# Hybrid attention/mLSTM block on one core: PSUM banks dealt out anew, weight tiles loaded two units ahead, gate products in four groups, small loads in another order

## The chip, the cores and the metric

The kernel runs on one core of one Trainium2 chip. The metric is the device time of one execution in microseconds (us). Of the kernel before there are three runs, with a median of 1435.84 us (1435.15 to 1436.73). One further execution was profiled. In this text PE is the matrix engine, DVE the vector engine, ACT the scalar engine, POOL the general-purpose engine and SP the engine that issues most DMAs.

## What is computed

One layer of a block with sequence length S = 1024 and width D = 1024, in float32. `x` is normalised (RMSNorm) and multiplied by one wide input matrix, whose columns feed two branches. Eight heads of differential attention: two softmaxes per head, with a bias that depends on the distance of the positions and a mask by chunks of 64, of which the second times lambda is taken from the first before the product with v. And eight heads of an mLSTM (a matrix memory with gates). Both are gated, projected, merged by per-channel gates, projected once more, added to `x` and normalised again. The attention, cut to what matters here:

```python
logits = jnp.einsum("pbhqd,pbhkd->pbhqk", qb, k).astype(jnp.float32) + bias
probs = jax.nn.softmax(jnp.where(mask, logits, NEG_INF), axis=-1)
attn = probs[0] - lam * probs[1]
return jnp.einsum("bhqk,bhkv->bhqv", attn, v)
```

## The kernel before

**Split numbers.** TensorE works on fp16 pairs. Each float32 operand is split into a high and a low half, and each product is three matmuls: L329 to L331 with 512 columns, where the weights stand still (q, k and others), and L358 to L360 with 256 columns, where `x` stands still.

**Units.** The input projection is cut into units of up to 256 weight columns. A unit's weights come from HBM in two halves of four k-chunks, `wt`, from a pool of WT = 3 tiles (L44, L223). `prep` (L234) sums their squares on ACT (L245), `fnorm_finish` (L155) turns the sum into a scale by way of a tiny matmul (L165) and a row of one-column DVE operations (L135 to L139), and the scaled halves are written as `wp` by ACT (L257) and DVE (L259). `start_load` asks for a unit's first half and `finish_load` for the second.

**The order.** Python generators write instructions down in an interleaved order, and a scheduler with the tile pools decides what finally stands in each engine's queue. The main loop (L1067 to L1116) goes through the units, and between a unit's matmuls it takes steps of a side job by a table of slots: PLAN_A for attention heads 0 to 6, PLAN_C for head 7, PLAN_M, PLAN_N and PLAN_Z for the mLSTM heads.

**An attention head** (L797). It has eight blocks of 128 queries. For block i and each of two halves, PE writes logits to `psb` (L812, one tile of two PSUM banks), DVE adds the bias BB and takes the extreme (L822), and ACT takes exp (L826). `combine` subtracts the two (L837 on DVE), and `turn` splits the result (L844 on ACT, L845 on DVE) and has a DMA on SP's queue transpose it (L847). `pv` (table names v0 to v7, L855 to L857) multiplies the transposed tile with v into `pvp`: blocks 0 to 3 fill one PSUM bank, and 4 to 7 the next one. ACT sums the squares of the result (L858), POOL makes a factor (L862 to L864, `fac`), and DVE reads the bank out, scaled by it (`on`, L870). `pvp` has one bank, so that v4 starts when L870 has read blocks 0 to 3. Q and K of the next head come from its own unit by way of `hl` (L599, L600) and four small DMAs each (L608, L610).

**Before the first head.** `x` arrives in eight tiles. ACT and DVE sum their squares (L383, L381), DVE scales them (L387), PE transposes them (L396, into `pmi`, two banks), and ACT and DVE write the pair X (L398, L399). The bias table `tb` is written to DRAM with one copy for each of 128 rows (`tb_d`, L432, 1.57 MB out of 8 partitions). A head's `strip` is read back from it (L584) and scaled by POOL (L585, L588), and DVE copies it into BB (L800). The input and forget gates of the mLSTM need 32 matmuls with a stationary operand of 32 columns (L468).

## Time and profile before

| what | value |
|---|---|
| three runs | 1435.84 us median (1435.15 to 1436.73) |
| the profiled execution | 1435.78 us, of which the span is 1433.9 us |
| PE busy | 1380.6 us (96% of the span) |
| DVE, ACT, POOL busy | 848.0, 735.0, 157.5 us |
| granted TensorE clock, mean | 0.995 |

The span runs from the first to the last instruction that the profile shows; 1.9 us of the execution lie outside it. In a list of instructions a row has its start, its duration, the engine and line, what is written and read, and in brackets the idle time of its engine just before it with what ended that. In the list of waits a row has the engine, the tile and line that waited, what it waited for, and then the total in us, the number of times and the longest.

### The profile page before, as it was taken

What the parts mean: (1) busy time and instruction counts of PE and PEld (TensorE: products, weight loads), DVE (VectorE), ACT (ScalarE), POOL (GpSimd) and SP (SyncE); (2) the same over time, 40 slices, a digit from 0 to 9 for tenths busy, and PEclk for the clock granted to TensorE, in tenths of its full rate; (3) what the DMA queues carried; (4) which work ended last, traced back from release to release, by engine and by line L of the source; (5) the groups of instructions that cost most, each with busy time, mean ns of one, the idle gap of its engine ahead of it and who ended that gap; (6) DMA issues with size and microseconds to landing.
All of it is one profiled execution on the core that took longest, in us unless ns stands there. A gap on an engine that the chain in (4) does not pass through costs nothing.

```text
span 1433.9 us, 25050 instructions
## 1 busy us (share of the span) xinstructions
PE 1380.6 (96%) x9650; PEld 913.3 (64%) x9650; DVE 848.0 (59%) x2310; ACT 735.0 (51%) x1533; POOL 157.5 (11%) x215
## 2 busy tenths in 40 slices
PE   6989999999999999999999999999999999999997
PEld 3656575665756655444486787778769675444786
DVE  6276868677686756533445674775866564233633
ACT  7276556565566667832353444443435344644542
POOL 2001010010100100100102020220211200122004
PEclk9999999999999999999999999999999999999999
DMA  6456355463554645543321313231232135534303
GB/s 200 68 142 140 83 107 124 104 141 82 114 121 91 136 95 130 163 149 125 96 74 60 104 31 101 47 87 47 66 97 75 60 86 158 168 103 162 118 16 118
DMA packets 232585, 150.14 MB, mean 105 GB/s; under 512 B 117297, under 2 KB 209730, under 8 KB 232466
## 3 DMA queue, kind: packets, MB, share of 16 engines
q1 hardware_dynamic: 218450, 123.28, 35.0%
q10 hardware_dynamic: 14016, 25.27, 5.3%
q8 instruction: 75, 1.23, 0.3%
q14 instruction: 44, 0.36, 0.1%
HBM read 90.12 MB, written 18.55 MB: 76 GB/s over the span
## 4 chain that ended last, share of the span: by engine, by line
PE 77%; DVE 9%; ACT 4%; DMA 4%; POOL 3%; issue 3%; SPq 0%; POOLq 0%; DVEq 0%; ACTq 0%
PE pp L329 14%; PE pp L331 14%; PE pp L330 14%; PE pp L360 8%; PE pp L358 8%; PE pp L359 8%; PE psb L812 3%; DVE z L822 3%; DMA z<-z 2%; ACT z L826 1%; DMA qw<-rows_d 1%; DVE wp L259 1%; PE psb L908 1%; PE pvp L855 1%; DVE hl L600 1%
## 5 line engine op out<-in xcount | busy, mean ns | idle before, releaser
L358 PE MATMUL pp<-wp,X 128*128 128x256 f16 x1280 | 349.7, 273 | 0.0
L359 PE MATMUL pp<-wp,X 128*128 128x256 f16 x1280 | 349.7, 273 | 0.0
L360 PE MATMUL pp<-wp,X 128*128 128x256 f16 x1280 | 349.7, 273 | 0.0
L329 PE MATMUL pp<-X,wp 128*128 128x512 f16 x768 | 291.7, 380 | 0.3 <-ACT wp L257 0.3
L331 PE MATMUL pp<-X,wp 128*128 128x512 f16 x768 | 291.3, 379 | 0.6 <-DVE wp L259 0.6
L330 PE MATMUL pp<-X,wp 128*128 128x512 f16 x768 | 291.8, 380 | 0.0
L257 ACT ACTIVATE wp<-wt,sb 128x512 f16<-128x512 f32 x208 | 136.9, 711 | 105.4 <-DVE sb L138 70.6
L331 PEld LDWEIGHTS <-wp 128*128 128x128 f16 x1024 | 100.0, 98 | 119.7 <-DVE wp L259 1.2
L245 ACT ACTIVATE junk<-wt 128x1024 bf16<-128x1024 f32 x112 | 118.1, 1055 | 100.0 <-DMA wt<-in_w_in_dram 89.7
L329 PEld LDWEIGHTS <-wp 128*128 128x128 f16 x1024 | 100.2, 98 | 103.0 <-issue 1.7
L330 PEld LDWEIGHTS <-wp 128*128 128x128 f16 x1024 | 100.1, 98 | 97.1
L259 DVE SCALAR_TENSOR_TENSOR wp<-wt,sb,wp 128x512 f16<-128x512 f32 x208 | 150.5, 760 | 14.4 <-ACT wp L257 12.8
L359 PEld LDWEIGHTS <-X 128*128 128x128 f16 x1280 | 125.3, 98 | 18.4 <-issue 2.4
L358 PEld LDWEIGHTS <-X 128*128 128x128 f16 x1280 | 125.4, 98 | 16.8 <-issue 0.8
L360 PEld LDWEIGHTS <-X 128*128 128x128 f16 x1280 | 125.3, 98 | 14.6
L826 ACT ACTIVATE z<-z,mx 128x256 f32<-128x256 f32 (+7 forms) x128 | 99.0, 773 | 61.7 <-DVE mx L825 46.1
L822 DVE CUSTOM_DVE_ANT_0 z<-psb,BB,negc 128x256 f32<-128x256 f32 (+7 forms) x128 | 104.1, 813 | 19.7 <-PE psb L812 19.4
L331 PE MATMUL pp<-Y,wp 128*128 128x512 f16 x256 | 97.1, 379 | 0.0
L330 PE MATMUL pp<-Y,wp 128*128 128x512 f16 x256 | 97.1, 379 | 0.0
L329 PE MATMUL pp<-Y,wp 128*128 128x512 f16 x256 | 97.1, 379 | 0.0
L649 DVE SCALAR_TENSOR_TENSOR acc<-up,wcol,acc 128x512 f32<-128x512 f32 x96 | 78.0, 827 | 27.4 <-POOL acc L650 24.5
L812 PE MATMUL psb<-K,Q 128*128 128x512 f16 (+3 forms) x384 | 83.5, 326 | 7.8 <-DMA K<-hl 4.6
(245 smaller groups left out, 2012.1 us busy)
## 6 DMA issues: line engine op xcount, KB each, us to landing
wt<-in_w_in_dram SPq DMA_DIRECT2D x128, 256.0 KB, 3.4
wt<-in_w_in_dram SPq DMA_DIRECT2D x24, 512.0 KB, 3.9
K<-hl SPq DMA_DIRECT2D x32, 256.0 KB, 3.7
gate_d<-tg ACTq DMA_DIRECT2D x32, 256.0 KB, 2.2
xt<-in_x_dram SPq DMA_DIRECT2D x8, 512.0 KB, 5.2
Q<-hl SPq DMA_DIRECT2D x32, 128.0 KB, 2.4
wt<-in_w_pa_dram SPq DMA_DIRECT2D x8, 512.0 KB, 5.4
ft<-gate_d ACTq DMA_DIRECT2D x16, 256.0 KB, 2.8
```

What stands on the lines that cost most here:

```text
L245: s.activation(j, w.wt[k], AF.Square, accum_out=ss[:, k:k + 1])
L257: s.activation(dst[0], src, AF.Copy, scale=w.sb)
L259: v.scalar_tensor_tensor(dst[1], src, w.sb, dst[0], op0=ALU.mult, op1=ALU.subtract)
L329: te.matmul(ps, wh, xh, start=(start and i == 0), stop=False, **kw)
L330: te.matmul(ps, wh, xl, start=False, stop=False, **kw)
L331: te.matmul(ps, wl, xh, start=False, stop=(stop and i == n - 1), **kw)
L358: te.matmul(ps[:, o], xh[:, t], wh, start=i == 0, stop=False)
L359: te.matmul(ps[:, o], xh[:, t], wl, start=False, stop=False)
L360: te.matmul(ps[:, o], xl[:, t], wh, start=False, stop=i == KC - 1)
L812: te.matmul(sp[:, c:e], Q[:, p, i * P:(i + 1) * P], K[p][:, j, c:e], start=(j == 0), stop=(j == 1))
L822: v.tensor_tensor_reduce(z[:, :n], sp[:, :n], bb[:, S - n:], negc, BIG, op0=ALU.add, op1=ALU.min, accum_out=mx)
L826: s.activation(z[:, :n], z[:, :n], AF.Exp, bias=mx, scale=-1.0, accum_out=rr[:, 2 * i + p:2 * i + p + 1])
```

## The change

- PSUM: `pmi` goes from two banks to one and `pvp` from one to two. The transposes of `x`, and in the mLSTM the small transposes and state products, take `pvp` instead of `pmi`.
- PLAN_A has v6 two slots and v7 four slots later in the table.
- Weights: WT goes from 3 to 6. The main loop finishes the load of the next unit and starts that of the one after it; unit 2 is loaded ahead of the main loop.
- `prep` waits five steps instead of two between the sums of squares and their use. For the first unit DVE takes one of the two sums, and of the first four tiles of `x` it takes tile 3 instead of tile 1.
- The strip is asked for and scaled after the four transfers of K. Its masked corner is written as 0 times strip plus a constant, without the tile `maskv`.
- The gate products go to four groups of 32 partitions of one PSUM bank, by half of the sequence and by high or low part of X. One ACT copy takes them out, the result goes to DRAM by ACT's queue, and `if_gates` loads six pieces instead of four and adds the two more on DVE.

Names in the diff: `te`, `s`, `v`, `g` are PE, ACT, DVE, POOL; `m_ps`, `v_ps`, `s_ps` take a tile of `pmi`, `pvp`, `psb`.

```diff
 RING = 15
-PLAN_A = [(0, 'q0'), (0, 'r0'), (0, 'q1'), (3, 'r1'), (4, 'q2'), (5, 'r2'), (9, 'q3'), (9, 'r3'), (9, 'q4'), (10, 'v0'), (14, 'v1'), (16, 'r4'), (17, 'q5'), (18, 'v2'), (19, 'r5'), (21, 'q6'), (24, 'r6'), (25, 'q7'), (27, 'r7'), (28, 'v3'), (29, 'v4'), (29, 'v5'), (30, 'f0'), (30, 'o0'), (31, 'v6'), (31, 'v7'), (42, 't0'), (55, 'f1'), (55, 'o1'), (55, 't1')]
+PLAN_A = [(0, 'q0'), (0, 'r0'), (0, 'q1'), (3, 'r1'), (4, 'q2'), (5, 'r2'), (9, 'q3'), (9, 'r3'), (9, 'q4'), (10, 'v0'), (14, 'v1'), (16, 'r4'), (17, 'q5'), (18, 'v2'), (19, 'r5'), (21, 'q6'), (24, 'r6'), (25, 'q7'), (27, 'r7'), (28, 'v3'), (29, 'v4'), (29, 'v5'), (30, 'f0'), (30, 'o0'), (33, 'v6'), (35, 'v7'), (42, 't0'), (55, 'f1'), (55, 'o1'), (55, 't1')]
...
 T2 = 5
-WT = 3
+WT = 6
 AHEAD = 2
...
     psb = ctx.enter_context(tc.tile_pool(name="psb", bufs=1, space=PSUM))
-    pmi = ctx.enter_context(tc.tile_pool(name="pmi", bufs=2, space=PSUM))
-    pvp = ctx.enter_context(tc.tile_pool(name="pvp", bufs=1, space=PSUM))
+    pmi = ctx.enter_context(tc.tile_pool(name="pmi", bufs=1, space=PSUM))
+    pvp = ctx.enter_context(tc.tile_pool(name="pvp", bufs=2, space=PSUM))
...
     g.memset(BB, 0.0)
-    maskv = ctile([64, 64], p="maskv")
-    g.memset(maskv, -(2.0 ** 100))
...
-    def prep(w, rowscale=None, keep=False):
+    def prep(w, rowscale=None, keep=False, alone=False):
         wd = w.width
...
         for k in range(2):
-            j = junk(4 * wd).rearrange("p (a b) -> p a b", a=4)
-            s.activation(j, w.wt[k], AF.Square, accum_out=ss[:, k:k + 1])
-            yield
-        yield
-        yield
+            if alone and k:
+                flat = w.wt[k].rearrange("p a b -> p (a b)")
+                v.tensor_tensor_reduce(main_tile("junk").bitcast(BF), flat, flat, 1.0, 0.0, op0=ALU.mult, op1=ALU.add,
+                                       accum_out=ss[:, k:k + 1])
+            else:
+                j = junk(4 * wd).rearrange("p (a b) -> p a b", a=4)
+                s.activation(j, w.wt[k], AF.Square, accum_out=ss[:, k:k + 1])
+            yield
+        for _ in range(5):
+            yield
         w.sb = sm(p="sb")
...
                 self.finish_load()
-                self.prepping = prep(self.w, self.rowscale and self.rowscale(), self.keep)
-                self.left = 16
+                self.prepping = prep(self.w, self.rowscale and self.rowscale(), self.keep, self is first)
...
             ss = sm(p="xss")
-            if tt in (1,):
+            if tt == (1 if th else 3):
                 v.tensor_tensor_reduce(main_tile("junk").bitcast(BF), xt, xt, 1.0, 0.0, op0=ALU.mult, op1=ALU.add, accum_out=ss)
...
                 X[th, kc // 2] = xtile("X")
-            tp = m_ps()
+            tp = v_ps()
             for tt in range(4):
-                te.transpose(tp[:, tt * P:(tt + 1) * P], xts[th * 4 + tt][:, kc * P:(kc + 1) * P], ident)
+                xb = xts[th * 4 + tt][:, kc * P:(kc + 1) * P]
+                te.transpose(tp[:, tt * P:(tt + 1) * P], xb, ident)
             hi, lo = x_src(kc, th)
...
     wsc = ctile([P, NT, H], p="wsc")
-    gif_d = dram.tile([32, S], F32, tag="gifd", name="gif_d")
+    gif_d = dram.tile([P, 512], F32, tag="gifd", name="gif_d")
...
             yield
-        t = R(shape=[32, S], p="gif")
-        for th in range(2):
-            gps = m_ps()
-            for i in range(KC):
+        t = R(shape=[P, 512], p="gif")
+        gps = s_ps()[:, :512]
+        for i in range(KC):
+            for th in range(2):
                 for k in range(2):
-                    te.matmul(gps[:32, :], parts[:, i, :], x_src(i, th)[k], start=(i + k == 0),
-                              stop=(i + k == KC))
-                yield
-            s.activation(t[:, HS[th]], gps[:32, :], AF.Copy, scale=sig[:32, :])
-        nc.sync.dma_start(gif_d, t)
+                    o = (th * 2 + k) * 32
+                    te.matmul(gps[o:o + 32, :], parts[:, i, :], x_src(i, th)[k], start=(i == 0), stop=(i == KC - 1))
+            yield
+        s.activation(t, gps, AF.Copy, scale=sig)
+        s.dma_start(gif_d, t)
         yield
...
         ff = R(shape=[H, NT, P], p="ff")
-        gl = [R(shape=[H, NT, P], p="gl") for _ in range(2)]
-        for k, dst in ((0, gi), (1, ff), (2, gl[0]), (3, gl[1])):
-            nc.sync.dma_start(dst.rearrange("h a b -> h (a b)"), gif_d[k * H:k * H + H, :])
+        gl = [R(shape=[H, NT, P], p="gl") for _ in range(4)]
+        for k, dst in ((0, gi), (1, ff), (2, gl[0]), (3, gl[1]), (4, gl[2]), (5, gl[3])):
+            r = k * H if k < 4 else 32 + (k - 4) * H
+            nc.sync.dma_start(dst.rearrange("h (t a) b -> h t (a b)", t=2),
+                              gif_d.rearrange("(t r) c -> r t c", t=2)[r:r + H])
         for _ in range(4):
...
             v.scalar_tensor_tensor(dst, dst, bif[:, k:k + 1], gl[k], op0=ALU.add, op1=ALU.add)
+            v.tensor_tensor(dst, dst, gl[2 + k], op=ALU.add)
         yield
...
         yield
-        cps = m_ps()
+        cps = v_ps()
         for k, t in enumerate((a, ws, en)):
...
         strip = ring.tile([P, 256], F32, tag="strip", name=nm("strip"), bufs=2)
-        nc.sync.dma_start(strip, tb_d[h, :P * 512].rearrange("(q u) -> q u", u=512)[:, 127:383])
-        g.tensor_scalar(strip, strip, invc, 1.0, op0=ALU.mult, op1=ALU.mult)
         mc = sm(p="mc")
-        v.tensor_scalar(mc, invc, 2.0 ** 20, None, op0=ALU.min)
-        g.tensor_scalar(strip[0:64, 192:256], maskv, mc[0:64, :], 1.0, op0=ALU.mult, op1=ALU.mult)
+        v.tensor_scalar(mc, invc, 2.0 ** 20, -(2.0 ** 100), op0=ALU.min, op1=ALU.mult)
+        def bias_strip():
+            nc.sync.dma_start(strip, tb_d[h, :P * 512].rearrange("(q u) -> q u", u=512)[:, 127:383])
+            g.tensor_scalar(strip, strip, invc, 1.0, op0=ALU.mult, op1=ALU.mult)
+            masked = strip[0:64, 192:256]
+            g.tensor_scalar(masked, masked, 0.0, mc[0:64, :], op0=ALU.mult, op1=ALU.add)
         Q = R(F16, [P, 2, S], p="Q")
...
                             nc.sync.dma_start(K[p][j * 64:j * 64 + 64, :, :], src)
+                if cb == 1:
+                    bias_strip()
         return None, post
...
             n = 4 - th
-            tp = m_ps()
+            tp = v_ps()
             for j in range(n):
...
         num = R(shape=[P, NT, P + 1], p="num")
-        st = sm(cols=48, p="st", bufs=2)
+        st = sm(cols=48, p="st", bufs=1)
         mv = sm(cols=16, p="mv", bufs=2).rearrange("p (c k) -> p c k", k=2)
...
-            cp = m_ps()[:, :P + 1]
+            cp = v_ps()[:, :P + 1]
             te.matmul(cp, kw[:, c, :], vr[:, c, :], start=True, stop=True)
...
     load_small()
+    order[2].finish_load()
...
                     if at + 1 < len(pq):
-                        pq[at + 1].start_load()
+                        pq[at + 1].finish_load()
+                    if at + 2 < len(pq):
+                        pq[at + 2].start_load()
                     if pq[at].prep_step():
```

**What moves.** Three places, each as it stands in an engine's queue before and after; the lines are those of each kernel, so that a line after the first edits has another number in the changed one.

PE in the attention of head 1, between the last product of block 3 with v (`z_1822` before, `z_1817` after) and the first of block 4 (`z_1845`, `z_1840`). Before; in the part left out there are 33 more products of 256 columns:

```order
L857 MATMUL pvp_1855<-vr_1290,z_1822 128x128
L358 MATMUL pp_2070<-wp_1813,X_256 128x256
...
L358 MATMUL pp_2070<-wp_1868,X_306 128x256
L855 MATMUL pvp_2097<-vr_1290,z_1845 128x128
```

After:

```order
L870 MATMUL pvp_1849<-vr_1289,z_1817 128x128
L360 MATMUL pp_2069<-wp_1858,X_247 128x256
L361 MATMUL pp_2069<-wp_1858,X_247 128x256
L362 MATMUL pp_2069<-wp_1858,X_247 128x256
L362 MATMUL pp_2069<-wp_1858,X_247 128x256
L868 MATMUL pvp_2096<-vr_1289,z_1840 128x128
```

Before, 37 products of 256 columns stand between blocks 3 and 4; now it is 6, and block 4 writes to another bank. Between the last logits of the head (block 7, second half) and the first product of block 7 with v there are 71 products of 256 columns both before and after, and 61 of the products with v before and 66 after; from the first logits of the head to that product there are 5 products of 256 columns fewer than before (72 instead of 77, in heads 1 to 5), and behind it 5 more.

DVE in the same head, from the logits of block 7 (first half) to the split of its transposed tile. Before:

```order
L822 ISA z_2003,mx_2004<-psb_1998,BB_95,negc_899 128x896
L822 ISA z_2022,mx_2023<-psb_2017,BB_95,negc_899 128x1024
L600 SCALAR_TENSOR_TENSOR hl_1880<-pp_1975,hl_1880 128x512
L837 SCALAR_TENSOR_TENSOR z_1984<-z_2003,nbeta_2008,z_1984 128x896
L822 ISA z_2038,mx_2039<-psb_2033,BB_95,negc_899 128x1024
L845 TENSOR_TENSOR z_2003<-z_1984,z_2003 128x896
L870 SCALAR_TENSOR_TENSOR on_2151<-pvp_1855,fac_2147,tz_1289 128x128 x2
L870 SCALAR_TENSOR_TENSOR on_2151<-pvp_1855,fac_2147,tz_1289 128x128
L870 SCALAR_TENSOR_TENSOR on_2151<-pvp_1855,fac_2147,tz_1289 128x128
L837 SCALAR_TENSOR_TENSOR z_2022<-z_2038,nbeta_2043,z_2022 128x1024
L548 SCALAR_TENSOR_TENSOR y_2328<-on_2151,y_2328 128x512
L845 TENSOR_TENSOR z_2038<-z_2022,z_2038 128x1024
```

After (L835 is L822 of before, L850 is L837, L858 is L845, L611 is L600, L883 is L870):

```order
L858 TENSOR_TENSOR z_1948<-z_1921,z_1948 128x768
L835 ISA z_2018,mx_2019<-psb_2013,BB_95,negc_898 128x1024
L850 SCALAR_TENSOR_TENSOR z_1980<-z_1999,nbeta_2004,z_1980 128x896
L835 ISA z_2034,mx_2035<-psb_2029,BB_95,negc_898 128x1024
L858 TENSOR_TENSOR z_1999<-z_1980,z_1999 128x896
L611 SCALAR_TENSOR_TENSOR hl_1873<-pp_1971,hl_1873 128x512
L883 SCALAR_TENSOR_TENSOR on_2153<-pvp_1849,fac_2149,tz_1288 128x128
L883 SCALAR_TENSOR_TENSOR on_2153<-pvp_1849,fac_2149,tz_1288 128x128
L850 SCALAR_TENSOR_TENSOR z_2018<-z_2034,nbeta_2039,z_2018 128x1024
L883 SCALAR_TENSOR_TENSOR on_2153<-pvp_1849,fac_2149,tz_1288 128x128 x2
L858 TENSOR_TENSOR z_2034<-z_2018,z_2034 128x1024
L556 SCALAR_TENSOR_TENSOR y_2326<-on_2153,y_2326 128x512
```

The split of block 5 (128x768) now stands ahead of block 7's logits, `hl` (128x512) behind the second half of them instead of ahead, two of the four L870 operations instead of four ahead of block 7's L837, and `y` (L548 before) behind its split. Before, the split of block 5 stands ahead of block 6's second half of logits.

SP's queue before the first head. Before:

```order
L409 DMA oh_333<-in_onehot_dram 32x384
L226 DMA wt_170<-in_w_in_dram 128x4x128 x2
L226 DMA wt_458<-in_w_in_dram 128x4x128 x2
L432 DMA tb_d<-tb_356 1024x1x384
L226 DMA wt_532<-in_w_in_dram 128x4x128 x2
L608 DMA Q_425<-hl_494 64x1024
L584 DMA strip_419<-tb_d 128x256
L608 DMA Q_425<-hl_494 64x1024 x3
L610 DMA K_426<-hl_535 64x2048 x2
L610 DMA K_427<-hl_535 64x2048 x2
L472 DMA gif_d<-gif_600 32x1024
L226 DMA wt_669<-in_w_in_dram 128x4x128 x2
```

After:

```order
L224 DMA wt_182<-in_w_in_dram 128x4x128 x2
L412 DMA oh_337<-in_onehot_dram 32x384
L224 DMA wt_459<-in_w_in_dram 128x4x128 x2
L224 DMA wt_668<-in_w_in_dram 128x4x128 x2
L435 DMA tb_d<-tb_360 1024x1x384
L619 DMA Q_426<-hl_482 64x1024 x4
L621 DMA K_427<-hl_530 64x2048 x2
L621 DMA K_428<-hl_530 64x2048 x2
L596 DMA strip_423<-tb_d 128x256
L224 DMA wt_671<-in_w_in_dram 128x4x128 x2
```

Four units' weights (eight tiles) are now issued ahead of `tb_d` where it was two and a half, no weights stand between `tb_d` and Q and K any more, and the strip goes behind K. In the attention of head 1 there were two transfers of K for the next head ahead of block 6's transpose and two between those of blocks 6 and 7; now none stands ahead, three between them and one behind.

## The prediction

> **What bounds the kernel now.** I read the page first: the share of each engine.
>
> ```profile
> PE 1380.6 (96%) x9650; PEld 913.3 (64%) x9650; DVE 848.0 (59%) x2310; ACT 735.0 (51%) x1533; POOL 157.5 (11%) x215
> ```
>
> PE is busy nearly throughout. The whole kernel can win at most the 53.3 us that PE idles (1433.9 - 1380.6), plus PE time that is itself slow. So I read the list of PE's waits next.
>
> ```profile
> PE pvp L855 <- DVE on L870: 12.0, 8, 1.6
> PE psb L812 <- DMA K<-hl: 4.6, 2, 2.5
> PE pvp L855 <- DMA z<-z: 4.2, 5, 1.1
> PE pmi L165 <- DVE s L159: 1.6, 7, 0.2
> ```
>
> The change touches all four of these rows: a second `pvp` bank (12.0), the order at the first K (4.6), later slots for v6 and v7 (4.2), a longer pause in `prep` (1.6). Together 22.4 us. Whether they are won depends on what is late next, which I take stage by stage. What the list has besides, the change leaves as it is.
>
> **The stage before the first head.** The rows of PE here, then those of the transfers behind them:
>
> ```profile
> L468 PE MATMUL pmi<-X,wifp x32: 378/379/388, 50.8 to 57.5; 128*32 128x512 f16 x32
> ```
> ```profile
> 50.80:58.00 7.20, 7.20 (x35) 3.17 (x35) 0.69 (x1) 0.60 (x1) 0.00 (x0) 1.00 0.52 67
> 36.00:68.00 32.00, 31.83 (x201) 19.23 (x199) 10.07 (x30) 7.37 (x13) 0.00 (x0) 1.00 0.49 59
> 77.00:86.00 9.00, 6.90 (x50) 5.40 (x49) 5.50 (x19) 6.92 (x17) 0.79 (x2) 0.69 0.89 235
> ```
> ```profile
> 74.23 0.16 PE L165 MATMUL pmi<-s,ones 128*128 128x1 bf16 x1 [0.50 <-ACT gif L471]
> 76.86 0.37 PE L812 MATMUL psb<-K,Q 128*128 128x128 f16 x2 [2.47 <-DMA K<-hl]
> 79.34 0.37 PE L812 MATMUL psb<-K,Q 128*128 128x128 f16 x2 [2.10 <-DMA K<-hl]
> 79.50 0.42 PE L358 MATMUL pp<-wp,X 128*128 128x256 f16 x1
> 79.72 0.42 PE L359 MATMUL pp<-wp,X 128*128 128x256 f16 x1
> 82.66 0.27 PE L358 MATMUL pp<-wp,X 128*128 128x256 f16 x1
> 82.77 0.27 PE L359 MATMUL pp<-wp,X 128*128 128x256 f16 x1
> ```
> ```profile
> 34.55 0.82 SPq L432 DMA_DIRECT2D tb_d<-tb  x1
> 45.11 8.08 SPq L226 DMA_DIRECT2D wt<-in_w_in_dram  x2
> 69.22 0.35 SPq L584 DMA_DIRECT2D strip<-tb_d  x1
> 69.67 2.21 SPq L608 DMA_DIRECT2D Q<-hl  x3
> 72.46 1.06 ACT L245 ACTIVATE junk<-wt 128x1024 bf16<-128x1024 f32 x1 [20.93 <-DMA wt<-in_w_in_dram]
> ```
>
> (The windows give stretch, length, busy time of PE, PEld, DVE, ACT and POOL, granted clock, DMA share and GB/s.) PE loses here: 7.0 us in the gate products (32 starts 0.216 apart, (57.5 - 50.8)/31), 0.50 at L165, 2.47 and 2.10 for K, and 1.5 in slow products: from 79.50 to 82.66 fifteen starts take 3.16 us where the step of 0.11 after 82.66 would need 1.65. Sum 13.6.
>
> K is late because of `tb_d`. From its issue at 34.55 until the strip that reads it goes out at 69.22, the DMA engines run at half load and 59 GB/s, and what is issued behind it waits: weights issued at 45.11 are there only at 72.46. The change takes Q and K out from behind the strip, but not out from behind `tb_d`, which stands ahead of them on SP's queue still.
>
> So the first step is when `tb_d` goes out. The rows at the start:
>
> ```profile
> 5.97 1.23 DVE L381 CUSTOM_DVE_ANT_0 junk<-xt 128x1024 bf16<-128x1024 f32 x1 [5.13 <-DMA xt<-in_x_dram]
> 11.56 0.75 DVE L387 TENSOR_SCALAR xt<-xt,xrs 128x1024 f32<-128x1024 f32 x1
> 13.03 0.75 DVE L387 TENSOR_SCALAR xt<-xt,xrs 128x1024 f32<-128x1024 f32 x1 [0.60 <-POOL xrs L386]
> 14.35 0.69 ACT L398 ACTIVATE X<-pmi,nws 128x512 f16<-128x512 f32 x1 [0.51 <-PE pmi L396]
> 17.32 0.61 PE L329 MATMUL pp<-X,wp 128*128 128x512 f16 x1 [0.26 <-ACT wp L257]
> ```
>
> DVE now sums the squares of `x` tile 3 and of half the first unit behind the scaling of tile 2 (11.56 to 12.3): 2 x 1.23, plus some 0.3 of one-column operations, so tile 3 is scaled at about 15.0 instead of 13.03. Its transposes, the first X (16.3 instead of 14.35) and the first product (about 19.0 instead of 17.32) follow: 1.7 us lost; two `pvp` banks and freer ACT could give it back later, so the bounds are 0 and 2.0. `tb` stands behind eleven pairs of X where it was ten, and ACT has the squares of two more units among them: I take 2.0 us later (1.5 to 5). Then `tb_d` is through at 71.2. Q (4 x 128 KB) and half of K (0.5 MB) need 4.5 us at the 235 GB/s of 77 to 86; with the half of the engines that `tb_d` leaves idle they may be half done by then, 2.2 us. I take 3.8: first K at 75.0.
>
> PE reaches that point at 74.39 less the 0.50 at L165 (its weights now come ahead of `tb_d`), plus 1.7, less what the gates save. Four groups of 32 columns at best run side by side: 7.0/4 = 1.8; at worst the 7.0 stay; I take 2.5, 4.5 saved, nearer the best since the four write different partitions and read one stationary operand. So PE arrives at 71.1 and waits 3.9 us. The second pair of logits now comes 51 products later (about 5.9 us) and K's second half is there by then. The slow products: two gaps of 2.5 and 2.1, with two short pairs of matmuls between, cost 1.5; for one gap of 3.9 I take 1.0. The Trainium skill ("TensorE: Matmul & The Clock Gate", Part 1) has the clock halve after an idle window of about 3.4 us that runs freely; here two gaps, each shorter, did it (0.69 granted). By the rule a gap of 3.9 would cost up to the same 1.5, without it nothing: the gain below would be 3.9 or 5.4.
>
> New losses: 2.5 + 1.7 + 3.9 + 1.0 = 9.1. The gain is 13.6 - 9.1 = **4.5** (0 to 9). Most of what the gates save is waited away again: while K ends last, their price hardly counts, and it would if K came early.
>
> **The heads.** PE's gaps in heads 0, 1 and 7, and head 1's chain on DVE:
>
> ```profile
> 123.95 0.22 PE L855 MATMUL pvp<-vr,z 128*128 128x128 f16 x1 [1.61 <-DVE on L870]
> 132.76 0.23 PE L855 MATMUL pvp<-vr,z 128*128 128x128 f16 x1 [1.14 <-DMA z<-z]
> 185.12 0.22 PE L855 MATMUL pvp<-vr,z 128*128 128x128 f16 x1 [1.59 <-DVE on L870]
> 193.86 0.23 PE L855 MATMUL pvp<-vr,z 128*128 128x128 f16 x1 [0.98 <-DMA z<-z]
> 191.27 0.16 PE L165 MATMUL pmi<-s,ones 128*128 128x1 bf16 x1 [0.24 <-DVE s L159]
> 492.13 0.22 PE L855 MATMUL pvp<-vr,z 128*128 128x128 f16 x1 [0.42 <-ACT junk L858]
> 547.53 0.22 PE L855 MATMUL pvp<-vr,z 128*128 128x128 f16 x1 [1.46 <-DVE on L870]
> ```
> ```profile
> 176.73 1.28 DVE L822 CUSTOM_DVE_ANT_0 z<-psb,BB,negc 128x1024 f32<-128x1024 f32 x1 [1.11 <-PE psb L812]
> 178.02 0.67 DVE L600 SCALAR_TENSOR_TENSOR hl<-pp,hl 128x512 f16<-128x512 f32 x1
> 181.12 1.09 DVE L845 TENSOR_TENSOR z<-z,z 128x896 f16<-128x896 f32 x1
> 183.75 0.61 DVE L870 SCALAR_TENSOR_TENSOR on<-pvp,fac,tz 128x128 f32<-128x128 f32 x2 [1.53 <-POOL fac L864]
> 187.65 1.23 DVE L845 TENSOR_TENSOR z<-z,z 128x1024 f16<-128x1024 f32 x1 [0.58 <-ACT z L844]
> ```
> ```profile
> 188.90 2.97 SPq L847 DMA_TRANSPOSE z<-z  x1
> ```
> ```profile
> 147.30:194.00 46.70, 43.43 (x309) 25.81 (x308) 39.49 (x115) 32.08 (x75) 3.13 (x5) 1.00 0.56 111
> ```
>
> With two banks v4 no longer waits for `on`. But v7 needs the transposed tile of block 7, which L845 at 187.65 makes and the DMA brings at 193.86, 5.0 us after its issue at 188.90. DVE is 39.49 us busy of the 46.7 from the head's first logits to v7, so v7 is bound by DVE's chain, not by PE's. If DVE's order stayed, all 1.59 would return as a longer wait at v7. DVE's order (front, second piece) does change, in heads 1 to 5: the split of block 5, about 0.95 by the 1.09 of the larger one, fills the idle 1.11 ahead of block 7's logits; `hl` (0.67) falls into the idle 1.53 ahead of L870; and one or two L870 (0.3) move behind L837. So the tile comes about 1.9 earlier relative to the head's start. The five products that moved behind v7 (5 x 0.11) take 0.55 of that, and L165's 0.24 is hidden: 1.9 - 0.55 + 0.24, about 1.6. Since ACT's exp and POOL's `fac` stand in that chain too, I take **1.4** a head (0.2 to the full 1.59 + 0.98 + 0.24 = 2.8), 7.0 for five heads. v7's wait for the DMA grows from about 1.0 to 1.5 to 2.
>
> In head 0 the new order has less DVE work between the first logits and v7 (splits of the next units have moved out), so there PE binds and both gaps go: 1.61 + 1.14 less a little, **2.5** (1.5 to 3). Head 6 keeps the count of its products and its DVE work, so only part of such a gap can go: **1.0** (0 to 2). Head 7 has no wait for a transpose, so nothing takes the place of its 1.46: **1.4** (1 to 1.9, with the 0.42).
>
> The rest, at nothing: POOL loses a tile's memset; the gates' two added DVE sums (about 1.1 each, by the row of 128x896) and two loads lie in the attention, far ahead of their use. Loading two units ahead moves the same bytes earlier, over DMA engines at 0.56 of their time. One `pmi` bank serves only L165 and the like. If that cover fails: 3 at most.
>
> **Sum.** 4.5 + 2.5 + 7.0 + 1.0 + 1.4 = 16.4. Of the profiled execution's 1435.78 (span 1433.9 and 1.9 outside, 0.06 from the median) that leaves 1419.4.
>
> **The rivals.**
> - *Everything is won.* K's packets slip past `tb_d` on idle engines (share 0.49 speaks for it; the weights' 20.93 us against), the first logits wait 1.5, and no clock is lost: start 13.6 - 5.7 = 7.9. v7's tile arrives in time: 2.8 x 5 + 2.8 + 2 + 1.9 = 20.7. Time 1407 to 1411 with some overlap lost. DVE's 39.49 of 46.7 speaks against.
> - *Gates not side by side, K early.* 4.5 of the 7.9 go, 3.4 remain: 1420.5 with the heads as forecast. The Trainium skill ("TensorEngine Tiling (Array Packing)", Key Properties and Restrictions) says that a change of tiling mode drains PE and that column tiling has no fast weight load, which speaks against this edit; "TensorE: Matmul & The Clock Gate" (Part 3) gives 2.38 times for three such groups, an estimate of 2.9 us instead of 7.0. No row here shows either.
> - *The heads give nothing.* DVE's chain is as long as before, and the 1.59 goes into v7's wait in heads 1 to 6: only 4.5 + 2.5 + 1.4 = 8.4 remain, 1427.4.
> - *The start gives nothing.* `tb_d` goes out 5 us or more later; 11.9 remain, 1423.9. Both together: 1432.
> - *Slower: K ahead of the last transpose.* Three transfers of K (0.75 MB) now stand between the transposes of blocks 6 and 7 on SP's queue. At the 111 GB/s of the head they take 6.8 us, at 235 GB/s 3.2. Should v7's tile wait for that, heads 1 to 6 lose 1.8 to 5.4 each net of the 1.4: 11 to 32, less the other 8.4: 1438 to 1459. It decides from a transpose delayed by about 2.8 us on. Against it: `hl` is done some 4 us ahead of the tile, and two such transfers stood there before without harm.
>
> **How the numbers follow.** Forecast 0.48; heads nothing 0.17; everything 0.14; start nothing, or gates' price, 0.11; both nothing 0.06; slower 0.04. A measurement of this kernel tells about 0.2%, 2.9 us, from no change. Both-nothing (1432) counts partly as the same: faster by more than that 0.89, same 0.07, slower 0.04. The range takes in 1411 (all won) and 1431 (short of both nothing).
>
> **What would show it.** Right: v4 without a wait for L870; v7 with 1.5 to 2 us for z<-z in heads 1 to 5; 32 gate products within 2 to 3 us; one gap for K of 3 to 5 us near 71 to 75; `tb_d` out near 36.5; first product near 19. Wrong: v7's gap above 3 us; first logits later than 77; L165 or `pmi` waits in the mLSTM.

## The result and the profile after

| | before | after |
|---|---|---|
| median of the runs, us | 1436.01 (1435.15 to 1436.73) | 1450.88 (1443.99 to 1452.55) |
| ratio to before, 95% interval | | 1.0095 (1.0079 to 1.0110) |
| profiled execution, us | 1435.78 | 1452.55 |
| its span, us | 1433.9 | 1450.8 |

The change makes the kernel slower, by about 15 us; 1419.4 was forecast. In the code after, line numbers have shifted: L825 is the logits (L812 before), L835 the maximum (L822), L868 the products with v (L855), L871 (L858) and L883 (L870) the accumulations behind them, L858 and L860 the last split and its transpose (L845, L847), L163 the column sum in `prep` (L165), L248 the squares of the weights on ACT (L245), L260 their split into pairs (L257), and in the mLSTM L921, L940, L943, L958, L960 and L964 (L908, L927, L930, L945, L947, L951).

The page's shares of the engines, after:

```profile
PE 1381.1 (95%) x9650; PEld 915.9 (63%) x9650; DVE 846.8 (58%) x2314; ACT 735.6 (51%) x1530; POOL 162.1 (11%) x214
```

PE is as busy as before, 1381.1 against 1380.6 us. By the page nearly the whole difference is idle time, and PE's waits say where (waited for; total us, times, longest; `issue` stands for time in which PE waited for nothing that the profile shows):

```profile
PE pvp L868 <- DMA z<-z: 8.1, 8, 2.6
...
PE psb L958 <- ACT num L964: 6.2, 5, 1.7
PE psb L960 <- DVE C L943: 5.6, 7, 0.9
PE psb L825 <- ACT tz L571: 4.8, 1, 4.8
...
PE psb L960 <- issue: 3.8, 3, 2.0
...
PE pmi L163 <- DVE s L157: 0.3, 1, 0.3
```

The 12.0 that v's products waited for DVE (L870) is gone, and so is nearly all of `pmi`'s 1.6. Three rows lie in none of the places where the prediction looks for a wait: 6.2, 5.6 and 3.8 at L958 and L960, in the mLSTM. Before, only one of the three was there, with 0.9 us (L947 for C). The rows of the mLSTM's scores, with the first and the last start in us ahead of the semicolon, date them (before, then after):

```profile
L908 PE MATMUL psb<-acc,acc x128: 272/275/356, 760.2 to 1172.4; 128*128 128x128 f32 x128
```
```profile
L921 PE MATMUL psb<-acc,acc x128: 272/275/356, 756.3 to 1188.5; 128*128 128x128 f32 x128
```

At the first score the new kernel is 3.9 us ahead; at the last it is 16.1 behind. The mLSTM has lost 20.0. Up to there the account goes by the start of the first logits of each head:

| head | 0 | 1 | 2 | 3 | 4 | 5 | 6 | 7 |
|---|---|---|---|---|---|---|---|---|
| before, us | 76.9 | 147.5 | 208.4 | 268.8 | 330.0 | 390.3 | 450.8 | 510.5 |
| after, us | 75.7 | 143.1 | 202.6 | 261.5 | 323.1 | 381.9 | 443.9 | 502.8 |
| gain so far | 1.2 | 4.4 | 5.8 | 7.3 | 6.9 | 8.4 | 6.9 | 7.7 |

So 4.4 of the 7.0 forecast up to head 1 came, 3.3 of the 8.0 forecast for heads 1 to 6, and from head 7 to the first score 3.8 were lost where 1.4 was to be won. Of the 16.4 forecast, 12.5 are missing at the first score; the mLSTM then takes 20.0 that were not forecast at all, and what stands behind it 0.8.

The mLSTM's loss starts in ACT's order. ACT after, just ahead of the first wait for `num`, and what PE then does:

```profile
764.73 1.93 ACT L260 ACTIVATE wp<-wt,sb 128x512 f16<-128x512 f32 x3
...
770.83 1.06 ACT L248 ACTIVATE junk<-wt 128x1024 bf16<-128x1024 f32 x1 [3.07 <-DMA wt<-in_w_in_dram]
...
773.89 1.06 ACT L248 ACTIVATE junk<-wt 128x1024 bf16<-128x1024 f32 x1 [1.92 <-DMA wt<-in_w_in_dram]
...
774.95 0.47 ACT L964 ACTIVATE num<-psb 128x387 f32<-128x387 f32 x1
```
```profile
775.47 0.49 PE L958 MATMUL psb<-vr,E 128*128 128x129 f32 x2 [1.58 <-ACT num L964]
```

The copy `num` frees the bank that PE waits for. It doesn't wait for PE (its row names no idle): it stands in ACT's queue behind two squares, and these wait for weights still in flight, 3.07 and 1.92 us. Before, the same copy followed its square with little room:

```profile
774.16 1.06 ACT L245 ACTIVATE junk<-wt 128x1024 bf16<-128x1024 f32 x1 [1.31 <-DMA wt<-in_w_in_dram]
...
775.69 0.49 ACT L951 ACTIVATE num<-psb 128x387 f32<-128x387 f32 x1 [0.38 <-PE psb L947]
```

There ACT waited 0.38 for PE; the squares' waits for DMA, present before too, cost nothing. That margin of 0.4 is what the change used up. What moved the squares back by more than that was the question for the experiments. In the change three things could: three more steps of pause in `prep` (five where there were two), six weight tiles loaded two units ahead, and the banks, one `pmi` and two `pvp`, with the new order.

### The profile page after: what moved, and what is told of

It is laid out like the page before. It is cut to its first block, busy times and chain, and to the rows that moved or that the text cites. A ratio compares the mean times of both kernels' runs of the same rounds, so it can differ in the third digit from the quotient of the medians.

```text
span 1450.8 us, 25032 instructions
## 1 busy us (share of the span) xinstructions
PE 1381.1 (95%) x9650; PEld 915.9 (63%) x9650; DVE 846.8 (58%) x2314; ACT 735.6 (51%) x1530; POOL 162.1 (11%) x214
## 4 chain that ended last, share of the span: by engine, by line
PE 69%; DVE 9%; ACT 6%; issue 6%; DMA 5%; POOL 2%; SPq 0%; POOLq 0%; DVEq 0%; ACTq 0%
PE pp L331 12%; PE pp L333 12%; PE pp L332 12%; PE pp L360 9%; PE pp L361 8%; PE pp L362 8%; PE psb L825 3%; DMA z<-z 3%; DVE z L835 2%; DVE acc L662 2%; DMA qw<-rows_d 1%; ACT z L839 1%; ACT wp L260 1%; POOL acc L663 1%; DVE z L858 1%
## 5 line engine op out<-in xcount | busy, mean ns | idle before, releaser
L260 ACT ACTIVATE wp<-wt,sb 128x512 f16<-128x512 f32 x208 | 136.0, 712 | 92.3 <-DVE sb L136 67.9
L248 ACT ACTIVATE junk<-wt 128x1024 bf16<-128x1024 f32 x111 | 117.2, 1056 | 93.6 <-DMA wt<-in_w_in_dram 83.1
L262 DVE SCALAR_TENSOR_TENSOR wp<-wt,sb,wp 128x512 f16<-128x512 f32 x208 | 146.8, 752 | 14.3 <-ACT wp L260 13.1
L835 DVE CUSTOM_DVE_ANT_0 z<-psb,BB,negc 128x256 f32<-128x256 f32 (+7 forms) x128 | 104.1, 813 | 16.0 <-PE psb L825 15.1
L825 PE MATMUL psb<-K,Q 128*128 128x512 f16 (+3 forms) x384 | 83.2, 325 | 9.2 <-ACT tz L571 4.8
```

Of the source, the lines that this page charges most:

```text
L248: s.activation(j, w.wt[k], AF.Square, accum_out=ss[:, k:k + 1])
L260: s.activation(dst[0], src, AF.Copy, scale=w.sb)
L262: v.scalar_tensor_tensor(dst[1], src, w.sb, dst[0], op0=ALU.mult, op1=ALU.subtract)
L825: te.matmul(sp[:, c:e], Q[:, p, i * P:(i + 1) * P], K[p][:, j, c:e], start=(j == 0), stop=(j == 1))
L835: v.tensor_tensor_reduce(z[:, :n], sp[:, :n], bb[:, S - n:], negc, BIG, op0=ALU.add, op1=ALU.min, accum_out=mx)
```

## The experiments

All are timed against the kernel before on the same chip (its medians there: 1435.52 to 1436.43 us); the ratios' 95% intervals are in brackets.

**The pause back to two steps** (all else as after).

```
-        for _ in range(5):
+        for _ in range(2):
             yield
```

> The changed kernel with the pause in prep back at two steps instead of five. Theory P (the pause makes wp late, so the slots of wt come free late, the loads and the sums of squares behind them arrive late on ACT, and the mLSTM's copy of num stands behind them): the five waits of L958 on num (6.2 us) and the seven of L960 on C (5.6 us) go, and with them some clock; 1428 to 1436. Theory W (the deeper weight queue puts the squares into the mLSTM's way, whatever the pause): no change, 1446 to 1452. Theory B (the mLSTM's small products in the pvp banks are the cause): no change either.

Measured: 1428.67 us, ratio 0.9948 [0.9933, 0.9963]: 22 us less than after. PE waits for nothing in the mLSTM; the window over most of it (stretch, length, busy PE, PEld, DVE, ACT, POOL, clock, DMA share, GB/s), after and then with the short pause:

```profile
690.00:1300.00 610.00, 594.39 (x4142) 417.12 (x4141) 334.50 (x948) 260.90 (x512) 76.97 (x87) 0.99 0.29 81
```
```profile
690.00:1300.00 610.00, 610.00 (x4246) 425.02 (x4245) 344.81 (x967) 271.54 (x534) 83.84 (x91) 1.00 0.30 84
```

In the heads the column sum now waits 9.2 us where it waited 0.3, and the wait for z falls from 8.1:

```profile
PE pmi L163 <- DVE s L157: 9.2, 7, 1.8
PE pvp L868 <- DMA z<-z: 3.5, 10, 0.9
```

Head 7 starts at 500.6, 2.2 ahead of after: even there the long pause wins nothing on balance. Of the 24.0 us between the two profiled spans (1450.8 and 1426.8), 21.3 lie between the first and the last score of the mLSTM.

**The weight tiles back to three** (loaded one unit ahead, pause of five).

```
-WT = 6
+WT = 3
...
-                        pq[at + 1].finish_load()
-                    if at + 2 < len(pq):
-                        pq[at + 2].start_load()
+                        pq[at + 1].start_load()
```

> The changed kernel with three weight tiles and the loads asked for as before. Theory W: the mLSTM's waits go, 1428 to 1436. Theory P: little changes there, 1445 to 1452. Theory B: no change. Before the first head the loads of units 2 and 3 stand behind the table again, so up to 3 us of the start's gain may be lost in any case.

Measured: 1449.32, 1.0089 [1.0072, 1.0106]. The mLSTM's waits stay (7.3, 5.6 and 3.1 us). The depth isn't the cause; what it does cost comes below.

**Both of these together.**

> The changed kernel with the pause at two and the weights as before, all else changed. Theories P and W, alone or together: 1422 to 1432, since the start (3.5 won in the trace) and the heads (about 5 won) stay. Theory B: 1445 or more.

Measured: 1429.94, 0.9958 [0.9944, 0.9973]: the pause alone decides; with the short pause the depth is worth 1.3 us or nothing.

**Only the banks and the order of v6 and v7, in the kernel before.**

```
-    pmi = ctx.enter_context(tc.tile_pool(name="pmi", bufs=2, space=PSUM))
-    pvp = ctx.enter_context(tc.tile_pool(name="pvp", bufs=1, space=PSUM))
+    pmi = ctx.enter_context(tc.tile_pool(name="pmi", bufs=1, space=PSUM))
+    pvp = ctx.enter_context(tc.tile_pool(name="pvp", bufs=2, space=PSUM))
...
-            tp = m_ps()
+            tp = v_ps()
```

> The kernel before with the PSUM banks of the change, its uses of them and its PLAN_A, nothing else. Theory B: 10 us slower or more, 1446 and up. Otherwise the heads' gain alone: 1424 to 1432, v4 without its wait for L870 and v7 waiting 1 to 2 us for its transposed tile.

Measured: 1428.78, 0.9948 [0.9933, 0.9963]. The banks lose nothing in the mLSTM, and these few lines alone win as much as the whole change with a short pause. Its waits show what they trade: `pvp` for DVE's 12.0 is gone, and

```profile
PE pmi L165 <- DVE s L159: 9.0, 7, 1.6
PE psb L812 <- DVE mx L822: 6.9, 11, 1.9
```

the column sum waits 9.0 where it waited 1.6. That PE comes to it earlier with v's waits gone fits, but was not tried by itself.

**The long pause in the mLSTM's units alone, and everywhere but there.**

```
+    5 if self.kind in ("mqk", "mz", "mvo", "gm") else 2
```
```
+    2 if self.kind in ("mqk", "mz", "mvo", "gm") else 5
```

> The changed kernel with five steps of pause only for the units of the mLSTM and its gate (mqk, mz, mvo, gm) and two for all others. Theory P (the pause delays, in the mLSTM, the weight split, the freeing of its tile, the next load and the sum of squares ahead of num): the loss comes back whole, 1444 to 1452, with L958 waiting for num and L960 for C. Rival H (the pause costs in the attention or before it, and the mLSTM only shows what is left over of it): 1427 to 1432.

> The changed kernel with five steps of pause for all units but those of the mLSTM, which have two. Theory P: 1426 to 1432, no waits for num or C in the mLSTM. Rival H: 1444 or more. Beside the kernel with two steps everywhere (1428.67) it also prices what the pause wins in the heads, where L163 then waits 9.2 us in all: up to 2.5 us won.

Measured: 1448.5, 1.0094 [1.0079, 1.0109], and 1430.61, 0.9962 [0.9950, 0.9975]. The long pause does its harm in the mLSTM's units. Outside them it wins nothing on balance: the column sum's wait is gone, but v7's wait for its transposed tile takes 11.1 us in heads 0 to 6.

**A pause of three.**

> The changed kernel with three steps of pause. One step is three products, 0.65 us in a unit of 512 columns. Theory P: the squares come 0.65 us later than with two steps; num had about 0.5 us of room there, so only small waits return, 1427 to 1434. If the time jumped back to 1446 or more, it would be another order on ACT that decides and not the delay.

Measured: 1429.98, 0.9961 [0.9948, 0.9974]. The cost doesn't grow evenly with the steps: one step more costs 1.3 us or nothing, three cost 22.2 (1450.88 against 1428.67). A pause of four was not tried.

**The squares of the mLSTM's units taken of X instead of the weights**, with the long pause there. The scales of these units then come from X; the squares keep their size and number, but need no transfer.

```
-                s.activation(j, w.wt[k], AF.Square, accum_out=ss[:, k:k + 1])
+                sq = w.wt[k] if pause < 5 else X[k, 0].rearrange("p a b c -> p (a b c)")[:, :4 * wd]...
+                s.activation(j, sq, AF.Square, accum_out=ss[:, k:k + 1])
```

> The kernel with five steps of pause in the mLSTM's units, in which those units' sums of squares read a half of X (always there, of the same size) instead of the weights. The scales come out otherwise, so the split is not the reference's; the time of each operation is the same. Theory P by way of ACT (the squares wait for the late load at the head of ACT's queue, and num and up stand behind them): the loss goes, 1427 to 1433. Theory P by another way (the late split itself, or its DVE operations, delays C and num): the loss stays, 1444 to 1452.

Measured: 1429.77, 0.9956 [0.9942, 0.9970]: the loss, 18.7 us beside the kernel with the long pause in these units, is gone, though the split and the load come as late against the products (L940 and its like at 765.19 here and 767.08 there). ACT and SP with the long pause (first list) and with X (second):

```profile
765.90 1.94 ACT L260 ACTIVATE wp<-wt,sb 128x512 f16<-128x512 f32 x3
768.09 2.58 SPq L224 DMA_DIRECT2D wt<-in_w_in_dram  x4
774.93 1.06 ACT L248 ACTIVATE junk<-wt 128x1024 bf16<-128x1024 f32 x1 [1.72 <-DMA wt<-in_w_in_dram]
775.99 0.47 ACT L965 ACTIVATE num<-psb 128x387 f32<-128x387 f32 x1
```
```profile
763.26 1.06 ACT L249 ACTIVATE junk<-X 128x1024 bf16<-128x1024 f16 x1
764.31 1.93 ACT L261 ACTIVATE wp<-wt,sb 128x512 f16<-128x512 f32 x3
766.50 2.57 SPq L224 DMA_DIRECT2D wt<-in_w_in_dram  x4
771.05 0.49 ACT L966 ACTIVATE num<-psb 128x387 f32<-128x387 f32 x1 [3.20 <-PE psb L962]
```

With X the copy waits 3.20 us for PE, and PE for nothing in the mLSTM. The squares did not keep their place: they now stand ahead of the splits in ACT's queue (763.26) and no longer between splits and `num`. So place and wait changed together. Either way the last link is shown: the late split and the late load cost nothing by themselves, and the pause is paid through squares that stand ahead of `num` in ACT's queue and wait there for a load.

**The gate products as before** (short pause): two halves in turn, 32 columns.

```
-                    te.matmul(gps[o:o + 32, :], parts[:, i, :], x_src(i, th)[k], start=(i == 0), stop=(i == KC - 1))
+                    te.matmul(gps[:32, :], parts[:, i, :], x_src(i, th)[k], start=(i + k == 0),
+                              stop=(i + k == KC))
```

> The changed kernel with two steps of pause and the gate products of before (32 products of 7.0 us instead of 1.9). If K ends last ahead of the first logits (5.3 us of waiting there with the new gates), most of the 5.1 us is taken from that wait: at most 1 us slower, 1428 to 1430. If the gates count in full: 1433 to 1435.

Measured: 1427.75, 0.9949 [0.9930, 0.9967], beside 1428.67 with the new ones: what the gates save is waited away, as the prediction said. PE waits 5.3 us ahead of the first logits with the new gate products and not at all with the old. The gates aren't all that differs, though: with the old ones 48 products of 256 columns and 3 of 512 more stand ahead of the first logits in PE's queue, some 5.9 us of work that covers a late K too.

**`tb_d` on ACT's queue and the strip on POOL's** (short pause), so that neither stands ahead of Q and K on SP's.

```
-        nc.sync.dma_start(tb_d.rearrange("h (q u) -> h q u", u=513)[:, :, :384],
+        s.dma_start(tb_d.rearrange("h (q u) -> h q u", u=513)[:, :, :384],
...
-            nc.sync.dma_start(strip, tb_d[h, :P * 512].rearrange("(q u) -> q u", u=512)[:, 127:383])
+            g.dma_start(strip, tb_d[h, :P * 512].rearrange("(q u) -> q u", u=512)[:, 127:383])
```

> The changed kernel with two steps of pause, the bias table written by ACT's queue and the strips read by POOL's. If Q and K of the first head are late because they stand behind the table on SP's queue, the 5.3 us that PE waits ahead of the first logits go down to what the strip leaves, and the time is 1422 to 1427. If the transfers share the engines in any queue, or the strip now ends last: 1427 to 1432.

Measured: 1435.0, 0.9997 [0.9987, 1.0006], 6 us worse than with one queue and worse than either expectation. The weights issued on SP meanwhile are held all the same. What costs PE its longest wait of the stage is another transfer, the strip, which now ends last: it goes out when `tb_d` has landed, DVE waits for it at the copy into BB, and ACT and PE wait behind DVE (SP's issues, DVE's copy, PE's wait):

```profile
48.21 19.70 SPq L224 DMA_DIRECT2D wt<-in_w_in_dram  x4
```
```profile
78.69 0.29 DVE L813 COPY BB<-strip 128x256 f32<-128x256 f32 x1 [23.42 <-POOL strip L599]
```
```profile
PE pp L360 <- DVE tz L572: 9.8, 1, 9.8
```

Four issues take 19.70 us while `tb_d` is in flight on another queue: transfers meet in the engines, not only in the queue. The Trainium skill ("DMA: Bandwidth & Descriptors", Issuing engines are not separate DMA queues) says the same, that they interleave on the same engines whoever issued them. PE's wait of 9.8 goes back to the strip; what another queue for `tb_d` alone would cost or win this run doesn't show.

**`tb_d` written with 128 rows outermost** (short pause): the 12 KB table goes to DRAM first, and the copies are made from there.

```
-        nc.sync.dma_start(tb_d.rearrange("h (q u) -> h q u", u=513)[:, :, :384],
-                    tb.unsqueeze(1).to_broadcast([H, P, 384]))
+        tb_0 = dram.tile([H, 384], F32, tag="tb0", name="tb_0")
+        nc.sync.dma_start(tb_0, tb)
+        nc.sync.dma_start(tb_d.rearrange("h (q u) -> q h u", u=513)[:, :, :384],
+                          tb_0.unsqueeze(0).to_broadcast([P, H, 384]))
```

> The changed kernel with two steps of pause and the table written in two steps: 12 KB to DRAM, and from there to the 128 rows with the rows outermost, so that the transfer is not bound to 8 source partitions. If the half of the engines that the table holds for 35 us is what delays K: the transfer takes about 18 us, the 5.3 us ahead of the first logits and the slow products behind them (1.5) go, 1421 to 1424. If it takes as long as before: 1428 to 1430.

Measured: 1420.14, 0.9893 [0.9878, 0.9908], 8.5 less than without and a little below the range expected. SP's issues:

```profile
36.02 0.29 SPq L436 DMA_DIRECT2D tb<-tb  x1
38.57 0.63 SPq L437 DMA_DIRECT2D tb_d<-tb  x1
...
50.54 0.34 SPq L598 DMA_DIRECT2D strip<-tb_d  x1
...
55.70 3.97 SPq L623 DMA_DIRECT2D K<-hl  x4
```

The windows (as above) while `tb_d` is in flight, after and then here:

```profile
37.00:70.00 33.00, 33.00 (x254) 21.96 (x252) 14.37 (x48) 11.31 (x20) 0.00 (x0) 1.00 0.51 62
```
```profile
37.00:55.00 18.00, 17.85 (x123) 9.30 (x121) 9.99 (x31) 8.94 (x16) 0.79 (x2) 1.00 0.79 180
```

From `tb_d`'s issue to the strip's, which needs it, are 12.0 us (50.54 - 38.57) instead of the 34.67 of before (69.22 - 34.55), and all transfers of the window together move 180 GB/s instead of 62. Nothing waits for K any more: its four transfers go out from 55.70 to 59.67 and take at most 4.4 us to land, ahead of the 67.9 (73.2 - 5.3) at which PE came to the first logits with the short pause alone. (These logits, too, stand some 5.9 us of products later now; K is early enough for either place.) The Trainium skill ("DMA: Bandwidth & Descriptors", Rules for kernel authors) names a reason: an outermost dimension below 16 confines a transfer to at most that many of the 16 engines, and the 128 partitions should ideally stand outermost. With 8 outermost the share was 0.51, half the engines; the rule agrees. The edit also reads the copies from DRAM instead of 8 partitions of SBUF, and this was not tried apart.

**The same table in the kernel with the banks alone.**

> The kernel before with the PSUM banks and PLAN_A of the change (1428.78) and the table written in two steps. There PE does not wait for K ahead of the first logits, so nothing is to be won from that: 1427 to 1430. What it has more than the kernel above is then the price of all other edits.

Measured: 1424.09, 0.9920 [0.9905, 0.9935]. It won 4.7 us over the banks alone, where little or nothing was expected: the table's transfer held back more there than the first K, which that kernel doesn't wait for. Between 40 and 90 us DVE's longest wait for a sum of squares of weights is 17.0 us with the banks alone and 2.2 with the wide table.

**The old gate products with the wide table** (the edit of the gates above, on the kernel with the wide table).

> The kernel with the table written in two steps and two steps of pause (1420.14), with the gate products of before. If the saving of 5.1 us was only hidden behind the late K: 1424 to 1426. If the gates are worth nothing here either (another transfer or the strip ends last): 1419.5 to 1421.5.

Measured: 1428.88, 0.9941 [0.9923, 0.9958], 8.7 more than with the new gates. With K early the gates' price counts: compared at equal work of PE, 5.7 of it are lost by the time of the first logits, near the 5.1 that the new gates save. The other 3.0 are lost in head 7, more than was expected and for no reason that was tried.

**K of heads 1 to 7 on ACT's queue** (long pause outside the mLSTM).

```
-                            nc.sync.dma_start(K[p][j * 64:j * 64 + 64, :, :], src)
+                            (s if h else nc.sync).dma_start(K[p][j * 64:j * 64 + 64, :, :], src)
```

> The changed kernel with five steps of pause in the attention and two in the mLSTM (1430.61), K of heads 1 to 7 sent by ACT's queue instead of SP's. If the transfers of K ahead of the last transpose on SP's queue make v7 late: waits for z<-z fall from 11.1 us to 5 or less, every head takes 59 us, 1424 to 1428. If the chain on the vector engine or the shared DMA engines do: waits for z<-z stay at 8 us or more, 1429 to 1433.

Measured: 1432.92, 0.9975 [0.9964, 0.9987]; v7's waits for z grow from 11.1 to

```profile
PE pvp L869 <- DMA z<-z: 14.5, 12, 2.1
```

So the transposes aren't late because K stands ahead of them on SP's queue. In this kernel v7's tile takes 7.2 to 8.3 us from the transpose's issue to the product in heads 1 to 6 (365.69 to 374.00 in head 4), longer than with K on SP's queue.

**The wide table with three weight tiles** (short pause).

> The kernel with the table written in two steps and two steps of pause (1420.14 with six weight tiles), with three weight tiles and the loads asked for as before. If the deeper queue costs 3 us in head 7 and helped the start only past the table: 1416 to 1419, no wait of L868 for junk in head 7. If the start needs the six tiles: 1420 to 1424.

Measured: 1418.96, 0.9884 [0.9868, 0.9901]: the fastest kernel of the study, 17 us under the one before. Beside the wide table with six tiles (1420.14) the ranges of the two runs' times overlap (1417.50 to 1420.22 and 1419.43 to 1421.60); the deeper queue is worth nothing here.

## Why the prediction was wrong, point by point

- **The pause, the step that failed.** The prediction counted the longer pause as a gain alone (L165's 0.24 a head) and put the rest at nothing, 3 at most; for the mLSTM it had no term. It asked what the pause hides in the heads, not who waits for what `prep` does later. The mLSTM lost 20.0 us. In the mLSTM the chain is: pause, then L163, the scale, the splits L260, the release of the weight tile, the next load, the squares of that load on ACT, and behind them in ACT's queue `num` and `up` (L347, ACT's copy of a unit's product), for which PE and DVE wait. In the profile after, against the one with the short pause, and counted from the same product (L940, at 765.90 and 763.93), the split starts at -1.2 instead of -5.1, the load goes out at +1.0 instead of -2.0, and the second square starts at +8.0 instead of +4.1. ACT with the short pause:

```profile
758.80 2.56 ACT L260 ACTIVATE wp<-wt,sb 128x512 f16<-128x512 f32 x4
...
768.01 1.06 ACT L248 ACTIVATE junk<-wt 128x1024 bf16<-128x1024 f32 x1 [0.98 <-DMA wt<-in_w_in_dram]
...
769.79 0.49 ACT L964 ACTIVATE num<-psb 128x387 f32<-128x387 f32 x1 [0.63 <-PE psb L960]
```

  At +5.9 `num` is needed (769.79 - 763.93): at +4.1 the square is out of its way, at +8.0 it isn't. By the pauses of 2, 3 and 5 and the squares of X, this is shown. Of the 20.0 lost, some 14 are the three waits (6.2 + 5.6 + 3.8, less the 0.9 of before and 0.7 behind the last score), and 2.9 are products at half clock, shown in the last section; the rest is not accounted for. The 5.6 and 3.8 at L960 fit `up`, which stands behind the same squares and holds DVE ahead of L943. How the 20 divide among these was not tried by itself.
- **What the profile had shown.** The squares' waits for DMA stood among the costliest groups of before, on an engine off the critical path; the prediction passed them over. The row that mattered was the 0.38 behind them. None of the prediction's signs of being wrong came (v7's gap stayed below 3 us, the first logits came before 77, no column sum and nothing else in `pmi` waited in the mLSTM): it looked for trouble only where it had looked for gains.
- **The rival in whose range the time fell.** *Slower: K ahead of the last transpose* had 1438 to 1459, and 1450.88 lies in it by luck. That rival has heads 1 to 6 lose 11 to 32 us; they won 3.3.
- **More tiles don't help**, against the picture of a deeper queue as a cover: three or six tiles, 1449.32 and 1450.88. The load of the next but one unit still waits until a tile is released by the late splits, and the square asked for is the one of that load.
- **The start and head 0**: 4.5 and 2.5 were forecast. The first logits came 1.2 earlier. Behind them, before lost another 2.1 at its second K and 1.5 in slow products, after only 1.3; so the start won some 3.5 (1.2 + 2.1 + 0.2). The marks held, the gates a little better than forecast: `tb_d` out at 36.61 (36.5), the first product at 18.74 (19.0), the gates in 1.91 us (2.5), one gap of 4.77 ending at 75.68 (3.9 near 75.0), slow products some 1.3 (1.0):

```profile
36.61 0.82 SPq L435 DMA_DIRECT2D tb_d<-tb  x1
```
```profile
18.74 0.63 PE L331 MATMUL pp<-X,wp 128*128 128x512 f16 x1
53.15 1.91 PE L473 MATMUL psb<-X,wifp 128*32 128x512 f16 x32
75.68 0.37 PE L825 MATMUL psb<-K,Q 128*128 128x128 f16 x2 [4.77 <-ACT tz L571]
129.15 0.23 PE L868 MATMUL pvp<-vr,z 128*128 128x128 f16 x1 [1.62 <-ACT wp L260]
```

  (The first gap's releaser is named `tz`, long done. That it is K, the last to land, is inferred; with the long pause outside the mLSTM alone the same gap, 4.3, is put down to K.) By these marks the prediction's own sum gives 4.2 for the start. The missing 0.7 fits the transposes of `x`, which now wait 3.6 for DVE to write X (L402) where it was 0.4. (In the prediction, the gain with and without a slower clock comes to 4.0 and 5.5 by its terms, not 3.9 and 5.4.)

  Head 0 won only 0.9 of the 2.5 (4.4 less 3.5). The forecast had PE bind there and both gaps go; v4's 1.61 went, but v7 waits 1.62 for its tile (last row) where it waited 1.14. The row names `wp`; with the long pause outside the mLSTM alone the same wait, 1.55, is put down to DMA z<-z.

  Four groups side by side took 1.91 us instead of 7.0, 3.7 times. That settles the rival in which they don't run side by side. The Trainium skill ("TensorE: Matmul & The Clock Gate", Part 3) has 2.38 for three groups, by which 2.9 was estimated; the measured number is better and decides. That the gates' price hardly counts while K ends last agrees with the runs (1427.75 with the old, 1428.67 with the new, the order of the first logits being another), and that it would if K came early is shown (1428.88 and 1420.14, in the same order).
- **The heads**: the mechanism was right, v4 no longer waits for `on`, and v7 does for its tile. Its wait is less even than the 1.5 to 2 forecast: 1.67, 0.77, 2.09, 0.92 and 2.56 in heads 1 to 5. Heads 1, 2 and 4 won 1.3 to 1.5 (1.4 forecast), head 6 0.8 (1.0). Heads 3 and 5 took 61.6 and 62.0 us, 0.4 and 1.5 more than before:

```profile
306.37 0.23 PE L868 MATMUL pvp<-vr,z 128*128 128x128 f16 x1 [2.09 <-DMA z<-z]
427.32 0.29 PE L868 MATMUL pvp<-vr,z 128*128 128x128 f16 x1 [2.56 <-DMA z<-z]
```
```profile
362.30 2.43 SPq L860 DMA_TRANSPOSE z<-z  x1
...
421.11 3.18 SPq L860 DMA_TRANSPOSE z<-z  x1
```
```profile
307.70:311.00 3.30, 3.30 (x20) 2.37 (x18) 0.68 (x3) 2.76 (x6) 1.49 (x3) 0.50 1.01 268
427.20:430.50 3.30, 3.18 (x27) 2.98 (x28) 0.95 (x2) 0.34 (x2) 0.00 (x0) 0.50 1.02 258
```

  The tile lands 6.2 us after its issue in head 5, where 5.0 was read off head 1. DVE's chain doesn't make it late: in heads 1 to 5 the transpose goes out 39.2 us after the head's first logits (421.11 - 381.93 in head 5, 362.30 - 323.13 in head 4; before 41.4 in head 1), 2.2 earlier where 1.9 was forecast. From there to v7 it is 5.3, 4.6, 5.7, 4.5 and 6.2 us. So it is the transposing transfer that differs, the term that the prediction read as 5.0. What delays it is not shown; the rival that made K on SP's queue responsible fell with K on ACT's. The second loss of heads 3 and 5 is the clock: behind their gaps of 2.09 and 2.56 it was 0.50 for the 3.3 us of each window above, which costs up to 1.6 a head, and the prediction had no term for it in the heads. With the short pause v7 waits only 3.5 in all, and L163 9.2: the pause just moves the wait.
- **Head 7**: forecast 1.4 won, measured 3.8 lost. From its first logits to the mLSTM's first score it takes 253.5 us, 249.7 before, and 249.4 with the long pause and three weight tiles: the deeper queue is the cause. ACT there waits for the weights of the next stage, whose row scaling it is given early by the deeper queue, and v's products wait behind it:

```profile
522.86 0.91 ACT L238 ACTIVATE wt<-wt,fa 128x256 f32<-128x256 f32 x2 [2.33 <-DMA wt<-in_w_pa_dram]
```
```profile
527.59 0.22 PE L868 MATMUL pvp<-vr,z 128*128 128x128 f16 x1 [1.74 <-ACT junk L871]
```

  With three tiles and the long pause L825 waits 1.3 us there once, and v's products not at all. It is the same pattern as in the mLSTM: an instruction that waits for a load at the head of ACT's queue.

## What to carry to other kernels

On an engine that takes its instructions in order, an instruction that waits for a DMA costs nothing only as long as nothing urgent stands behind it; read the idle time of the next urgent one (here 0.38 us) as the margin, and hold every edit that delays a release against it. Follow a step that is moved later through all that it releases, to the next load and to the first reader of that load, in every stage where the code runs and not only in the one that it was put in for. Where a transfer runs at half the engines' load, look at its outermost dimension before moving it between queues. Ask of each gap that is left on PE whether the clock stays up behind it.

## What the hardware showed that was not expected

The prediction read off the start of before that two gaps of 2.5 and 2.1 us, with little work between, slow the clock. After the change one gap of 2 us was enough: 2.09 and 2.56 in heads 3 and 5 were each followed by 3.3 us and more at 0.50, while 1.67 in head 1 and 1.74 in head 7 were followed by 1.00. In the mLSTM it was a gap of 2.03; one of 0.82 came behind it, but the clock is at 0.50 from 1079.1 on, ahead of that one's end. PE after, and the window behind it, granted clock 0.55:

```profile
1078.36 0.46 PE L960 MATMUL psb<-C,qw 128*128 128x129 f32 x2 [2.03 <-issue]
...
1080.17 0.80 PE L960 MATMUL psb<-C,qw 128*128 128x129 f32 x2 [0.82 <-DVE C L943]
```
```profile
1080.00:1086.50 6.50, 6.33 (x26) 3.94 (x27) 4.58 (x14) 1.61 (x3) 0.85 (x3) 0.55 0.00 0
```

Products at half speed follow: up to 1085.88 products of 256 columns start 0.21 apart, behind it 0.11. Of these 5.7 us half, some 2.9, is lost, as much as the two gaps themselves.
